# Key norms of the RWKV preparation: one addition and one power for both halves of the features

## The chip, the cores and the metric

The program runs on one core of a Trainium2 chip. The time is that of one execution on the device, in microseconds (us); a kernel's time is the median of its runs. The core's engines work side by side, each through its own list of instructions in a fixed order, and wait for each other through semaphores: TensorE (PE in the profile; PEld are its weight loads), VectorE (DVE), ScalarE (ACT), GpSimd (POOL) and SyncE (SP), which here issues most DMA transfers. The clock of TensorE is not constant: the profile gives, for each stretch, the share of the full clock that was granted.

## What is computed

The reference is one layer of a decoder trunk for 1024 tokens and 16 meta tokens, D_MODEL 1024. An input projection feeds four groups of heads (pooling, RWKV-7, a gated linear recurrence, an mLSTM), each 256 features wide; an output projection and a layer norm follow, then an MLP with a squared ReLU and 4096 hidden features, and a last layer norm. The part that matters here is RWKV's, with 4 heads of 64 features:

```python
def rwkv7_mixer(p, mu, w0, w_up, a0, a_up, g_up, k_k, k_a, r_k, gn_g, gn_b, v_first, v_mix):
    pm = p + (token_shift(p) - p) * mu
    r, k, v, wd, ad, gd = jnp.split(pm, RW_SPLITS, axis=-1)
    w = -jax.nn.softplus(-(w0 + jnp.tanh(wd) @ w_up)) - 0.5
    log_decay = -jnp.exp(w.astype(jnp.float32))
    a = jax.nn.sigmoid(a0 + ad @ a_up)
    ...
    kk = split_heads(k * k_k)
    kk = kk * lax.rsqrt(jnp.sum(kk * kk, -1, keepdims=True) + 1e-12)
    k = k * (1.0 + (a - 1.0) * k_a)
    ...
    bvec = kk * ah
    # step over the tokens: S = S * d - (S kk) b + v k ; y = S r
    ...
    bonus = jnp.sum(rh * kh * r_k, -1, keepdims=True) * vh
    out = (y + bonus.reshape(B, T, GROUP_W)) * g
```

The key norm is the line with `rsqrt`: for each token and head, the sum of 64 squares, plus 1e-12, to the power -0.5. `kk` is multiplied by it.

## The kernel before

Features lie on the 128 partitions and tokens along the free axis, so the 256 features of RWKV are two halves, f = 0 and 1, of 128 partitions, with two heads each. The tokens come in four blocks of 256; block 0 has the 16 meta tokens ahead of them, so 272 columns. Within a block the scan works on chunks of 128 tokens (block 0 has a third chunk, of 16).

All matrix products in float32 are done as three products of rounded parts: a high part (`whi`, made by ScalarE, L127 or L132) and the rest (`wlo`, made by VectorE, L128 or L133). Lines L476 to L478 are the input projection, which the code calls a sweep, L1169 to L1171 the output projection W_out, and L1191 the products of the MLP, whose second half writes to `bank`. L188 are transposes on TensorE.

The program is written as steps in a string (`PLAN`, L41 and below): `P2`, for one, is `rwkv_pre` of block 2, `I2` the inverse of its chunks' triangular matrices, `C2.0` a chunk's scan, `c2.0` that chunk's output (`rwkv_out`), `W2.1` a piece of W_out, `G` and `D` pieces of the MLP. A scheduler takes these steps as priorities and sets the order of the instructions on each engine with costs of its own; so an edit in one step can move instructions of other steps that run near it, and sometimes later ones. Tiles come from pools with a fixed number of buffers: a new tile of a name waits until the last reader of the oldest one of that name is done.

`rwkv_pre` (L604 and below) prepares a block. A first loop over f makes the decays: matmuls L626 and L627, tanh (L633, L638), L634 and the scan L635. A second loop over f does the rest of the half's work:

- L643 multiplies k by its gain (ScalarE), L645 squares it into `rw_s`, and L648 sums the squares over each head on TensorE: the squares are the stationary operand and a matrix of ones (`blk`, 2 columns) the moving one, so that tokens come to lie on partitions and the result is 128x2 for each chunk, 128x4 for the block's two chunks.
- `rsqrt` adds 1e-12 on VectorE (L139) and takes the power -0.5 on GpSimd (L140). In block 0 the meta chunk has an addition and a power of its own, 16x2.
- L657 brings the norm back to features on partitions: a matmul with the norm, broadcast to 64 columns, as its stationary operand and the identity as the moving one. L659 multiplies it into `kk` (VectorE).
- L661 and L662 are exponentials of the decays. L667 and L668 update k (the first writes an `rw_s`), L670 is r times k (another `rw_s`), L672 the matmul that sums it for the bonus, L673 and L674 the bonus. L675 to L683 multiply `kk`, r, k and a by the decays. L694 are the first matmuls behind, of the inverse.

Two things tie these together. `rw_s` has two buffers, and each half takes three in turn: the squares, L667's and L670's. And the tag `r` of PSUM, with two buffers, holds the sums of squares, the broadcast norms and L672's result in turn.

The head norms of the chunks' outputs use `rsqrt` as well (tile `rw_rs`). `rwkv_out` (L887 and below) then transposes the normalised output (L890), multiplies it by the gate's matmul (L892) in L895 and L896 into a tile `ys`, which has one buffer, and sends it to DRAM as `yd` (L591, issued by SP).

## Time and profile before

| | us |
|---|---|
| median of 3 runs | 1275.45 |
| lowest and highest run | 1268.3, 1279.51 |
| the profiled execution | 1273.62 |
| its span, first to last instruction | 1271.8 |
| TensorE busy in the span | 1208.1 |
| VectorE busy | 844.4 |
| ScalarE busy | 594.5 |
| GpSimd busy | 110.1 |

The mean granted clock of TensorE over the span was 0.983 of the full one. A row of a timeline has start, length, engine, line, operation, tiles and shapes, and in brackets the idle time ahead of it and what ended it: `[1.46 <-POOL rw_rn L140]` says that the engine stood still for 1.46 us until GpSimd's power on `rw_rn` was done. A row of the waits has the engine and line that waited, what it waited for, the total, the number of times and the longest. A group's row has shapes, count, busy time in us and mean of one in ns. A row of the windows has the stretch and its length, the busy time and count of each engine (TensorE, its weight loads, VectorE, ScalarE, GpSimd), the granted clock, the share of the DMA engines and GB/s. `rwkv_pre` runs at about 75 us (block 0), 187 (block 1), 481 (block 2) and 586 (block 3).

### The profile page before, as it was taken

The numbers are of one execution on the slowest core, as the hardware profiler recorded it, in microseconds if no ns is written. First come the engines' busy times: TensorE is split into PE (matmuls) and PEld (weight loads), VectorE is DVE, ScalarE is ACT, GpSimd is POOL, SyncE is SP. The second block draws the span as 40 slices with busy tenths as digits, with TensorE's granted clock in tenths as the row PEclk, the third lists the DMA queues.
The fourth block names the chain that finished last, engine by engine and source line by source line (L and its number), as shares of the span: only waits on it lengthen the run. The fifth ranks groups of instructions, "written<-read, shape, count | busy, mean of one in ns | idle before, by whom it ended". The sixth has DMA issues, their size and how long they took to land.

```text
span 1271.8 us, 20464 instructions
## 1 busy us (share of the span) xinstructions
PE 1208.1 (95%) x7642; PEld 1036.5 (81%) x7642; DVE 844.4 (66%) x1834; ACT 594.5 (47%) x989; POOL 110.1 (9%) x124
## 2 busy tenths in 40 slices
PE   4999999899987998999999899999999999999997
PEld 3989878889887996776788787888888888888886
DVE  8856476877743756736766789766765556445687
ACT  5433757354265534344343346655655543343330
POOL 4110010200120000001001330000000000000022
PEclk9999999899998998999999999999999999999999
DMA  7536333984895472565647767666666788666662
GB/s 250 183 106 227 94 124 93 204 202 105 232 285 158 147 291 88 159 157 129 224 117 210 254 228 235 224 233 241 221 237 231 237 296 283 198 192 191 193 220 100
DMA packets 123171, 247.90 MB, mean 195 GB/s; under 512 B 28832, under 2 KB 35632, under 8 KB 122944
## 3 DMA queue, kind: packets, MB, share of 16 engines
q1 hardware_dynamic: 114624, 229.82, 54.3%
q0 software_dynamic: 8448, 16.78, 7.8%
q8 instruction: 60, 0.98, 0.3%
q14 instruction: 39, 0.32, 0.1%
HBM read 195.17 MB, written 84.94 MB: 220 GB/s over the span
## 4 chain that ended last, share of the span: by engine, by line
PE 75%; DVE 8%; DMA 7%; issue 4%; ACT 4%; POOL 2%; SPq 1%; DVEq 0%; ACTq 0%; POOLq 0%
PE bank L1191 39%; PE b L1191 6%; PE b L477 5%; PE b L478 4%; PE b L476 4%; DMA wraw<-in_w_out 2%; DVE wlo L128 2%; PE r L694 2%; PE b L1170 1%; PE b L1169 1%; PE b L1171 1%; DMA wraw<-in_w 1%; ACT whi L127 1%; DMA yd<-ml_num 1%; POOL rw_rn L140 1%
## 5 line engine op out<-in xcount | busy, mean ns | idle before, releaser
L476 PE MATMUL b<-hTh,whi 128*128 128x256 f32 (+1 forms) x672 | 198.2, 295 | 3.2 <-ACT whi L127 2.3
L133 DVE TENSOR_TENSOR wlo<-wraw,whi 128x1024 fp32r<-128x1024 f32 x112 | 133.7, 1227 | 100.0 <-ACT whi L132 97.6
L477 PE MATMUL b<-hTl,whi 128*128 128x256 f32 (+1 forms) x672 | 198.3, 295 | 0.8 <-DVE hTl L133 0.7
L478 PE MATMUL b<-hTh,wlo 128*128 128x256 f32 (+1 forms) x672 | 196.7, 293 | 2.2 <-DVE wlo L128 2.1
L132 ACT CAST whi<-wraw 128x1024 fp32r<-128x1024 f32 x112 | 113.1, 1052 | 162.9 <-PE bank L1191 143.1
L1191 PE MATMUL bank<-whi 128*128 128x512 f32 x448 | 175.0, 392 | 2.6 <-DVE ys L896 2.6
L1191 PE MATMUL bank<-wlo,whi 128*128 128x512 f32 x448 | 175.6, 392 | 1.3 <-DVE wlo L133 1.3
L1191 PE MATMUL bank<-whi,wlo 128*128 128x512 f32 x448 | 175.3, 391 | 0.0
L127 ACT CAST whi<-wraw 128x1024 fp32r<-128x1024 f32 x90 | 94.3, 1048 | 144.5 <-PE b L477 49.6
L128 DVE TENSOR_TENSOR wlo<-wraw,whi 128x1024 fp32r<-128x1024 f32 x90 | 111.0, 1235 | 76.1 <-ACT whi L127 75.6
L476 PEld LDWEIGHTS b<-hTh,whi 128*128 128x128 f32 x672 | 131.6, 196 | 6.2 <-ACT whi L127 2.7
L478 PEld LDWEIGHTS b<-hTh,wlo 128*128 128x128 f32 x672 | 131.8, 196 | 4.5 <-DVE wlo L128 3.2
L477 PEld LDWEIGHTS b<-hTl,whi 128*128 128x128 f32 x672 | 131.7, 196 | 2.9 <-DVE hTl L133 1.4
L1191 PEld LDWEIGHTS bank<-whi 128*128 128x128 f32 x448 | 84.6, 189 | 20.0 <-issue 3.0
L1191 PEld LDWEIGHTS bank<-wlo,whi 128*128 128x128 f32 x448 | 84.5, 189 | 19.1 <-DVE wlo L133 1.9
L1191 PEld LDWEIGHTS bank<-whi,wlo 128*128 128x128 f32 x448 | 84.5, 189 | 17.4
L140 POOL TENSOR_TENSOR ln_rs<-ln_rs,mhalf 128x1 f32<-128x1 f32 (+1 forms) x22 | 32.8, 1495 | 611.1 <-DVE ln_rs L139 611.0
L1170 PE MATMUL b<-wlo,mixh 128*128 128x256 f32 x256 | 74.3, 292 | 3.4 <-DVE wlo L128 3.4
L1169 PE MATMUL b<-whi,mixh 128*128 128x256 f32 x256 | 73.3, 289 | 0.9 <-ACT mixh L132 0.9
L1171 PE MATMUL b<-whi,mixl 128*128 128x256 f32 x256 | 72.6, 287 | 0.0
L1170 PEld LDWEIGHTS b<-wlo,mixh 128*128 128x128 f32 x256 | 48.8, 191 | 6.5 <-DVE wlo L128 5.3
L1191 PE MATMUL b<-h1Th,wlo 128*128 128x512 f32 x128 | 52.3, 411 | 0.5 <-DVE wlo L128 0.5
(435 smaller groups left out, 2480.7 us busy)
## 6 DMA issues: line engine op xcount, KB each, us to landing
wraw<-in_w SPq DMA_DIRECT2D x48, 512.0 KB, 4.7
wraw<-in_w_in SPq DMA_DIRECT2D x42, 512.0 KB, 4.7
rd<-in_w POOLq DMA_DIRECT2D x16, 1024.0 KB, 13.5
wraw<-in_w_out SPq DMA_DIRECT2D x32, 512.0 KB, 4.7
wraw<-rd SPq DMA_DIRECT2D x64, 256.0 KB, 4.3
md<-m SPq DMA_DIRECT2D x48, 256.0 KB, 2.3
wraw<-md SPq DMA_DIRECT2D x48, 256.0 KB, 3.4
wraw<-in_w SPq DMA_DIRECT2D x48, 256.0 KB, 4.1
```

The lines of the kernel that those rows point to most:

```text
L127: nc.scalar.copy(hi, raw)
L128: (nc.gpsimd if pool else nc.vector).tensor_tensor(lo, raw, hi.bitcast(F32), op=ALU.subtract)
L132: self.nc.scalar.copy(hi, src)
L133: self.nc.vector.tensor_tensor(lo, src, hi.bitcast(F32), op=ALU.subtract)
L140: self.last_pool = nc.gpsimd.tensor_tensor(out, out, self.mhalf[0:rows, 0:w], op=ALU.pow).ins
L476: nc.tensor.matmul(pt, lhsT=wh[:, ks], rhs=hh[:, kt, 0:nb], start=(kt == 0), stop=False)
L477: nc.tensor.matmul(pt, lhsT=wh[:, ks], rhs=hl[:, kt, 0:nb], start=False, stop=False)
L478: nc.tensor.matmul(pt, lhsT=wl[:, ks], rhs=hh[:, kt, 0:nb], start=False, stop=(kt == 7))
L1169: nc.tensor.matmul(pt, lhsT=xh, rhs=wh, start=(kt == 0), stop=False)
L1170: nc.tensor.matmul(pt, lhsT=xh, rhs=wl, start=False, stop=False)
L1171: nc.tensor.matmul(pt, lhsT=xl, rhs=wh, start=False, stop=(kt == 7))
L1191: mm = lambda *p, **k: self.nc.tensor.matmul(*p, skip_group_check=True, **k)
```

## The change

The second loop of `rwkv_pre` is cut in two. A new loop over f does L643, the square and the sums of squares for both halves, into one PSUM tile `pn` with a further dimension of 2. Behind it stand one addition and one power for all four heads, into one tile `rw_rn` with 4 columns a chunk (128x8 in a block, 16x4 for block 0's meta chunk). The remaining loop reads its two columns from that tile. Lines behind the change stand one further down (L648 becomes L647, L657 becomes L658, L694 becomes L695).

```diff
--- before.py
+++ after.py
@@ -636,25 +636,26 @@
             cs.append(sg)
 
             nc.scalar.activation(at[:, f, 0:nb], pa, AF.Tanh, scale=0.5, bias=self.hp[:, 2 + f:3 + f])
+        m = 1 if mo else 0
+        pn = self.ps("r", [P, nch, 2, 2])
+        for f in range(2):
+            KK = kk[:, f, 0:nb]
+            nc.scalar.activation(KK, k[:, f, 0:nb], AF.Identity, scale=self.p("kk", f))
+            sq = self.rwp.tile([P, NBM], F32, name="rw_s", bufs=2)
+            nc.scalar.activation(sq[:, 0:nb], KK, AF.Square)
+            for ci, (c0, L, _, _) in enumerate(ch):
+                nc.tensor.matmul(pn[0:L, ci, f], lhsT=sq[:, c0:c0 + L], rhs=self.blk, start=True, stop=True)
+        rn = self.smp.tile([P, NTB + 1, 4], F32, name="rw_rn")
+        for rs, i0, i1 in ([(slice(0, NM), 0, 1)] if mo else []) + [(slice(0, P), m, nch)]:
+            self.rsqrt(rn[rs, i0:i1].rearrange("p a b -> p (a b)"), pn[rs, i0:i1].rearrange("p a b c -> p (a b c)"), 1e-12)
         for f in range(2):
             c = cs[f]
             A = at[:, f, 0:nb]
             K, R, V, KK, BV = (t[:, f, 0:nb] for t in (k, r, v, kk, bv))
-            nc.scalar.activation(KK, K, AF.Identity, scale=self.p("kk", f))
-            sq = self.rwp.tile([P, NBM], F32, name="rw_s", bufs=2)
-            nc.scalar.activation(sq[:, 0:nb], KK, AF.Square)
-            pn = self.ps("r", [P, nch, 2])
-            for ci, (c0, L, _, _) in enumerate(ch):
-                nc.tensor.matmul(pn[0:L, ci], lhsT=sq[:, c0:c0 + L], rhs=self.blk, start=True, stop=True)
-            rn = self.smp.tile([P, NTB + 1, 2], F32, name="rw_rn")
-            m = 1 if mo else 0
-            for rs, i0, i1 in ([(slice(0, NM), 0, 1)] if mo else []) + [(slice(0, P), m, nch)]:
-                o = rn[rs, i0:i1].rearrange("p a b -> p (a b)")
-                self.rsqrt(o, pn[rs, i0:i1].rearrange("p a b -> p (a b)"), 1e-12)
             pb = self.ps("r", [P, nb])
             for ci, (c0, L, _, _) in enumerate(ch):
                 for j in range(2):
-                    nc.tensor.matmul(pb[64 * j:64 * j + 64, c0:c0 + L], lhsT=rn[0:L, ci, j:j + 1].broadcast_to([L, 64]),
+                    nc.tensor.matmul(pb[64 * j:64 * j + 64, c0:c0 + L], lhsT=rn[0:L, ci, 2 * f + j:2 * f + j + 1].broadcast_to([L, 64]),
                                      rhs=self.ident[0:L, 0:L], start=True, stop=True)
             nc.vector.tensor_tensor(KK, KK, pb, op=ALU.mult)
             ep, en = tmp[:, 2], tmp[:, 3]
```

The order of instructions moves at these places. First TensorE, block 2 (about 481 to 489 us in the profile of before): the norm's sums of squares, the broadcasts of the norm, the bonus sums (written into `r`) and the transposes of the MLP's input (L188) between them. Before:

```order
L648 MATMUL r_5789<-cst_280,rw_s_5787 128x2 x2
L188 MATMUL b_6183<-cst_280,x_6174 128x128 x4
L188 MATMUL b_6192<-cst_280,x_6190 128x128
L934 MATMUL l_5860<-cst_280,ml_g_4376 128x8 x2
L188 MATMUL b_6192<-cst_280,x_6190 128x128 x3
L657 MATMUL r_5795<-cst_280,rw_rn_5792 64x128 x4
L672 MATMUL r_5809<-rw_s_5807,bd_rkb_949 128x256
L188 MATMUL b_6199<-cst_280,x_6190 128x128 x4
L648 MATMUL r_5821<-cst_280,rw_s_5819 128x2 x2
L657 MATMUL r_5827<-cst_280,rw_rn_5824 64x128 x4
L672 MATMUL r_5841<-rw_s_5839,bd_rkb_949 128x256
```

And with the change:

```order
L647 MATMUL r_5776<-cst_280,rw_s_5778 128x2 x2
L647 MATMUL r_5776<-cst_280,rw_s_5783 128x2 x2
L188 MATMUL b_6169<-cst_280,x_6160 128x128 x4
L188 MATMUL b_6178<-cst_280,x_6176 128x128
L935 MATMUL l_5846<-cst_280,ml_g_4366 128x8 x2
L188 MATMUL b_6178<-cst_280,x_6176 128x128 x3
L658 MATMUL r_5790<-cst_280,rw_rn_5787 64x128 x4
L673 MATMUL r_5804<-rw_s_5802,bd_rkb_949 128x256
L658 MATMUL r_5813<-cst_280,rw_rn_5787 64x128 x4
L673 MATMUL r_5827<-rw_s_5825,bd_rkb_949 128x256
```

Both halves' sums of squares now stand together ahead of the covering transposes, and one group of four transposes (the one on `b_6199`) no longer stands between the two halves; it comes behind the first eight matmuls of the inverse.

VectorE at the same place. `rw_s` written from `rw_a` is L667 (L668 with the change), `rw_s` from `rw_r` is L670 (L671). Before, between the additions and multiplications of block 2's norm:

```order
L659 TENSOR_TENSOR rw_kk_5760<-rw_kk_5760,r_5795 128x256
L673 TENSOR_TENSOR rw_bv_5762<-r_5809,rw_v_4871 128x256
L675 SCALAR_TENSOR_TENSOR rw_a_5761<-rw_a_5761,rw_kk_5760 128x256
L139 TENSOR_SCALAR rw_rn_5824<-r_5821 128x4
L677 TENSOR_TENSOR rw_kk_5760<-rw_kk_5760,p4_5767 128x256
L683 SCALAR_TENSOR_TENSOR rw_a_5761<-rw_a_5761,p4_5767 128x256
L667 TENSOR_SCALAR rw_s_5836<-rw_a_5761,hp_404 128x256
L659 TENSOR_TENSOR rw_kk_5760<-rw_kk_5760,r_5827 128x256
L668 SCALAR_TENSOR_TENSOR rw_k_4869<-rw_s_5836,rw_k_4869 128x256
L675 SCALAR_TENSOR_TENSOR rw_a_5761<-rw_a_5761,rw_kk_5760 128x256
L670 TENSOR_TENSOR rw_s_5839<-rw_r_4870,rw_k_4869 128x256
```

With the change:

```order
L668 TENSOR_SCALAR rw_s_5799<-rw_a_5751,hp_404 128x256
L944 TENSOR_TENSOR ml_li_5837<-l_5846,ifb_951 128x8
L669 SCALAR_TENSOR_TENSOR rw_k_4859<-rw_s_5799,rw_k_4859 128x256
L660 TENSOR_TENSOR rw_kk_5750<-rw_kk_5750,r_5790 128x256
L671 TENSOR_TENSOR rw_s_5802<-rw_r_4860,rw_k_4859 128x256
L676 SCALAR_TENSOR_TENSOR rw_a_5751<-rw_a_5751,rw_kk_5750 128x256
L680 TENSOR_TENSOR rw_r_4860<-rw_r_4860,p4_5757 128x256
L674 TENSOR_TENSOR rw_bv_5752<-r_5804,rw_v_4861 128x256
L678 TENSOR_TENSOR rw_kk_5750<-rw_kk_5750,p4_5757 128x256
L682 TENSOR_TENSOR rw_k_4859<-rw_k_4859,p4_5757 128x256
L684 SCALAR_TENSOR_TENSOR rw_a_5751<-rw_a_5751,p4_5757 128x256
L660 TENSOR_TENSOR rw_kk_5750<-rw_kk_5750,r_5813 128x256
```

Behind these rows follow, for half 1, L668, L945 (a small one), L669, L676 and L671. What moved in is half 0's own work on k and r: L668, L669, L671, L680 and L682 with `p4_5757`. Before, these five stood some 30 to 70 rows ahead, between input projections; three of them:

```order
L670 TENSOR_TENSOR rw_s_5807<-rw_r_4870,rw_k_4869 128x256
L521 COPY rw_q_5504<-rcar_291 128x1
L521 COPY rw_q_5540<-rcar_291 128x1
L679 TENSOR_TENSOR rw_r_4870<-rw_r_4870,p4_5767 128x256
L681 TENSOR_TENSOR rw_k_4869<-rw_k_4869,p4_5767 128x256
```

The third place is the end of block 3, VectorE at about 691 to 703 us: the last two `rwkv_out` (L895 and L896 on two tiles `ys`), the head norm's addition L139 and multiplication L914, sums of W_out (L1174) and splits of weights (L128). Before:

```order
L895 SCALAR_TENSOR_TENSOR ys_7650<-r_7645,prm_282,rw_bv_6663 128x128
L139 TENSOR_SCALAR rw_rs_7336<-rw_sm_7335 128x4
L895 SCALAR_TENSOR_TENSOR ys_7650<-r_7645,prm_282,rw_bv_6663 128x128
L914 TENSOR_TENSOR rw_yn_7337<-rw_yn_7337,rw_rs_7336 128x256
L896 TENSOR_TENSOR ys_7650<-ys_7650,r_7645 128x256
L1174 SCALAR_TENSOR_TENSOR x_7817<-x_7817,b_7963 128x256
L1174 SCALAR_TENSOR_TENSOR x_7819<-x_7819,b_7964 128x256
L128 TENSOR_TENSOR wlo_8062<-wraw_8059,whi_8061 128x1024
L895 SCALAR_TENSOR_TENSOR ys_7890<-r_7885,prm_282,rw_bv_6663 128x128 x2
L128 TENSOR_TENSOR wlo_8233<-wraw_8230,whi_8232 128x1024
L896 TENSOR_TENSOR ys_7890<-ys_7890,r_7885 128x256
```

With the change:

```order
L896 SCALAR_TENSOR_TENSOR ys_7632<-r_7627,prm_282,rw_bv_6649 128x128 x2
L913 TENSOR_REDUCE rw_sm_7317<-SA_7320 128x4
L897 TENSOR_TENSOR ys_7632<-ys_7632,r_7627 128x256
L139 TENSOR_SCALAR rw_rs_7318<-rw_sm_7317 128x4
L128 TENSOR_TENSOR wlo_8014<-wraw_8011,whi_8013 128x1024
L915 TENSOR_TENSOR rw_yn_7319<-rw_yn_7319,rw_rs_7318 128x256
L1175 SCALAR_TENSOR_TENSOR x_7799<-x_7799,b_7945 128x256
L896 SCALAR_TENSOR_TENSOR ys_7872<-r_7867,prm_282,rw_bv_6649 128x128 x2
L1175 SCALAR_TENSOR_TENSOR x_7801<-x_7801,b_7946 128x256
L897 TENSOR_TENSOR ys_7872<-ys_7872,r_7867 128x256
L128 TENSOR_TENSOR wlo_8044<-wraw_8041,whi_8043 128x1024
L128 TENSOR_TENSOR wlo_8215<-wraw_8212,whi_8214 128x1024
```

The first tile's L897 now stands ahead of the head norm's addition and multiplication, and the last tile's L896 and L897 ahead of both splits of weights. From about 785 us to the end TensorE's order is the one of before.

## The prediction

> **What bounds the kernel now.** I read the page first, then TensorE's waits, then the timeline of each place where one of those waits is for the key norm, and last the windows with the granted clock. The head of the page, the busy shares and the chain by line:
>
> ```profile
> span 1271.8 us, 20464 instructions
> PE 1208.1 (95%) x7642; PEld 1036.5 (81%) x7642; DVE 844.4 (66%) x1834; ACT 594.5 (47%) x989; POOL 110.1 (9%) x124
> PE bank L1191 39%; PE b L1191 6%; PE b L477 5%; PE b L478 4%; PE b L476 4%; DMA wraw<-in_w_out 2%; DVE wlo L128 2%; PE r L694 2%; PE b L1170 1%; PE b L1169 1%; PE b L1171 1%; DMA wraw<-in_w 1%; ACT whi L127 1%; DMA yd<-ml_num 1%; POOL rw_rn L140 1%
> ```
>
> TensorE is busy 1208.1 of 1271.8 us, so all idle time of TensorE in the whole program is 63.7 us, and only work that TensorE waits for can be won or lost. VectorE at 66% and GpSimd at 9% have room. The norm's power (L140 on `rw_rn`) has 1% of the chain. TensorE's waits for it, first in the whole run, then in the windows 66 to 86 us (block 0), 184 to 200 (block 1), 478 to 500 (block 2, with a second wait that stands beside it) and 580 to 600 (block 3); the columns are total, times and longest:
>
> ```profile
> PE r L657 <- POOL rw_rn L140: 5.0, 8, 1.5
> PE r L657 <- POOL rw_rn L140: 1.3, 3, 0.5
> PE r L657 <- POOL rw_rn L140: 1.2, 2, 0.8
> PE r L672 <- DVE rw_s L670: 1.6, 1, 1.6
> PE r L657 <- POOL rw_rn L140: 1.5, 1, 1.5
> PE r L657 <- POOL rw_rn L140: 1.1, 2, 0.7
> ```
>
> So 5.0 us of TensorE's time wait for the powers, and with the wait for L670 in block 2 some 6.6 us, 0.5% of the span. That is the ceiling of what the change can win in these four places; a measurement of this kernel tells about 1% from no change, 12.7 us.
>
> **The change, part by part: the instructions removed.** Per block one addition on VectorE and one power on GpSimd go (in block 0 two of each, because the 16 meta columns have their own). The remaining power has twice the columns: 128x8, in block 0 also 16x4.
>
> ```profile
> L139 DVE TENSOR_SCALAR rw_rn<-r x10: 142/156/163, 74.9 to 590.4; 128x4 f32<-128x4 f32 x8, 16x2 f32<-16x2 f32 x2
> L140 POOL TENSOR_TENSOR rw_rn<-rw_rn,mhalf x10: 692/1144/1492, 75.1 to 590.6; 128x4 f32<-128x4 f32 x8, 16x2 f32<-16x2 f32 x2
> L140 POOL TENSOR_TENSOR rw_rn<-rw_rn,mhalf 128x4 f32<-128x4 f32 x8 | 9.8, 1224 | 45.5 <-DVE rw_rn L139 45.5
> L140 POOL TENSOR_TENSOR ln_rs<-ln_rs,mhalf 128x1 f32<-128x1 f32 x21 | 32.3, 1540 | 610.7 <-DVE ln_rs L139 610.6
> L140 POOL TENSOR_TENSOR ln_rs<-ln_rs,mhalf 16x1 f32<-16x1 f32 x1 | 0.5, 542 | 0.4 <-DVE ln_rs L139 0.4
> ```
>
> Five additions of 0.156 us (0.8 us of VectorE) and five powers of about 1.1 us (5.5 us of GpSimd) go. Both engines have idle time around them, so this pays only through the waits. The trace has no 128x8 power. It is bounded from below by one 128x4, 1.22 us, and from above by two of them, 2.45. Width seems to cost something among the short ones (16x1 takes 0.54, the shortest of all, a 16x2, 0.69: 0.15 a column), and nothing in the 128x1, which at 1.54 is longer than the 128x4. I take 1.6: the 128x4 and four columns at 0.1, below the slope of the short ones because of the 128x1 row. The 16x4 gets 0.69 + 2 x 0.15 = 1.0.
>
> [...]
>
> **Block 0.** TensorE's norm matmuls (L648), the first cover behind them, and the two broadcasts of half 0:
>
> ```profile
> 74.13 0.74 PE L648 MATMUL r<-cst,rw_s 128*16 128x2 f32 x6
> 74.73 0.37 PE L476 MATMUL b<-hTh,whi 128*128 128x272 f32 x1
> 75.88 0.29 PE L657 MATMUL r<-cst,rw_rn 16*64 16x16 f32 x4 [0.41 <-POOL rw_rn L140]
> 77.35 0.66 PE L657 MATMUL r<-cst,rw_rn 128*64 128x128 f32 x8 [0.53 <-POOL rw_rn L140]
> ```
>
> Before, three waits make 1.3, two of them here. The first power (0.69) ended at 75.88, so it began 0.46 behind the norms. After, both halves' L647 stand together (0.6 us each, to 75.3); the powers then run from 75.8 to 76.8 (16x4) and 78.4 (128x8). Six matmuls cover the norm where four took from 74.73 to 75.47, 0.74 us; six make 1.1, to 76.4. The waits are then 0.4, and, behind a broadcast of 0.3, 1.3: 1.7 against 1.3. The second half's broadcasts wait for nothing. **+0.4 us**, ends 0 (the powers at 1.2) and +1.2 (at 2.45).
>
> **Block 1.** Two waits (1.2 together, the longer 0.8) become one, longer by the power's 0.4: 0.8 + 0.4 = 1.2. The order of ScalarE here gets one more table load, of the length of the first row below, in a stretch whose idle time just behind is the second row's 1.12:
>
> ```profile
> 188.62 1.28 ACT L1092 ACT_TABLE_LOAD   x1
> 197.96 0.47 ACT L1092 ACTIVATE sc<-l,prm 128x256 f32<-128x256 f32 x1 [1.12 <-PE l L1091]
> ```
>
> The 1.12 hide all but 0.2 of the 1.28: **+0.2 us**, ends -0.4 (a short power, the load hidden) and +1.3 (the load not hidden).
>
> **Block 2.** Here half 0's work on K, r and the bonus (L667, L668, L670, L679, L681) ran early in the old order, since the two `rw_s` buffers were free for it. Now both buffers hold squares until the norm matmuls have read them, so these five operations stand behind the norm, in VectorE's stream between the two halves. The old filling work, the old stalls and VectorE's pace:
>
> ```profile
> 483.94 0.60 PE L188 MATMUL b<-cst,x 128*128 128x128 f32 x4
> 486.34 0.66 PE L657 MATMUL r<-cst,rw_rn 128*64 128x128 f32 x8 [1.46 <-POOL rw_rn L140]
> 488.62 1.15 PE L672 MATMUL r<-rw_s,bd_rkb 128*128 128x256 f32 x2 [1.62 <-DVE rw_s L670]
> 483.52 0.42 DVE L659 TENSOR_TENSOR rw_kk<-rw_kk,r 128x256 f32<-128x256 f32 x1 [0.36 <-PE r L657]
> 487.04 0.42 DVE L659 TENSOR_TENSOR rw_kk<-rw_kk,r 128x256 f32<-128x256 f32 x1 [1.03 <-PE r L657]
> 488.05 0.42 DVE L670 TENSOR_TENSOR rw_s<-rw_r,rw_k 128x256 f32<-128x256 f32 x1
> ```
>
> From 487.04 to 488.05 three operations start, 0.335 us apart. Before, the second L670 set the second L672 at 488.62. After, the first broadcast comes 0.4 later (the longer power), so the first L660 is at about 483.95. From it to the second L671 the new order has thirteen full operations and one small, like the addition: 12 x 0.335 + 0.16 + 0.42 = 4.6, which ends at 488.55. So the second wait for the power is gone, but VectorE arrives when it did: the stall changes its releaser, not its end. What differs is that the four transposes (L188, 0.6 us), which filled TensorE between the halves, now stand behind both: **+0.6 us**, ends 0 (VectorE keeps ahead) and +1.5 (the power at 2.45).
>
> **Block 3.** Two waits (0.7 and 0.4) become one of 0.7 + 0.4: **0**.
>
> **The tail of block 3.** From about 690 us the planner writes W_out, the down products and the last two `rwkv_out` in another order. VectorE's rows, SP's issue and TensorE's wait:
>
> ```profile
> 692.93 0.43 DVE L914 TENSOR_TENSOR rw_yn<-rw_yn,rw_rs 128x256 f32<-128x256 f32 x1 [0.90 <-POOL rw_rs L140]
> 693.27 0.42 DVE L896 TENSOR_TENSOR ys<-ys,r 128x256 f32<-128x256 f32 x1
> 693.72 0.38 SPq L591 DMA_DIRECT2D yd<-ys  x1
> 700.33 0.61 DVE L895 SCALAR_TENSOR_TENSOR ys<-r,prm,rw_bv 128x128 f32<-128x128 f32 x2 [4.84 <-DMA yd<-ys]
> 700.97 1.23 DVE L128 TENSOR_TENSOR wlo<-wraw,whi 128x1024 fp32r<-128x1024 f32 x1
> 702.67 0.47 PE L1191 MATMUL bank<-whi 128*128 128x512 f32 x1 [2.56 <-DVE ys L896]
> ```
>
> The single `ys` buffer is sent out at 693.72 and free at 700.33, 6.6 us later. VectorE then does L895, a weight split (1.23) and L896, and TensorE waits 2.56 us for that. In the new order the earlier tile's product comes ahead of the wait for the head norm's power (0.90 + 0.34 sooner), and the last product ahead of the split (1.23; a sum of W_out, as long as an L914, takes its place: 0.8 sooner): 2.0 of 2.56 us. The down product that waited now also has more W_out matmuls ahead of it, but the loads on SP move with it, so I take **-1.5 us**, ends 0 and -2.6.
>
> Sum: 0.4 + 0.2 + 0.6 + 0 - 1.5 = -0.3. Against the profiled execution's 1273.62 us (span 1271.8 and 1.8 around it) that is 1273.3. The median of the three runs is 1275.45, 1.8 above the profiled one, and they spread from 1268.3 to 1279.51, wider than any term here.
>
> **The rivals.** Two rest on the clock, so first its rows: 488 to 492 us, 492 to 496, 496 to 500, and 704 to 707; the clock is the number ahead of the last two.
>
> ```profile
> 488.00:492.00 4.00, 3.14 (x10) 1.97 (x10) 3.33 (x11) 0.88 (x3) 0.00 (x0) 0.58 0.00 0
> 492.00:496.00 4.00, 3.73 (x19) 3.51 (x20) 2.03 (x8) 2.03 (x6) 0.00 (x0) 0.50 0.12 22
> 496.00:500.00 4.00, 4.00 (x15) 2.89 (x14) 3.35 (x13) 1.45 (x3) 0.00 (x0) 0.64 0.38 108
> 704.00:707.00 3.00, 3.00 (x8) 2.31 (x7) 2.96 (x6) 0.98 (x1) 1.27 (x1) 0.50 0.63 206
> 703.45 0.40 PE L1191 MATMUL bank<-whi 128*128 128x512 f32 x1
> 703.68 0.59 PE L1191 MATMUL bank<-wlo,whi 128*128 128x512 f32 x1
> 704.50 0.63 PE L1191 MATMUL bank<-whi 128*128 128x512 f32 x1
> 704.92 0.63 PE L1191 MATMUL bank<-wlo,whi 128*128 128x512 f32 x1
> ```
>
> After block 2's two stalls the clock is at half for about 3.4 + 4 + 2.9 = 10.2 us; after the tail's stall for some 3.4. A 512-column matmul then starts every 0.42 us instead of 0.23, so half of the time is lost at most: 1.6 us in the short stretch, 4.7 in the long one.
>
> *Slower: the merged waits bring the clock down elsewhere.* In blocks 0, 1 and 3 a single longer wait stands where there were two or three short ones. Block 2's stalls, 3.1 us within 4 us, were followed by half clock. If a merged wait of 1.1 to 1.3 us in one piece does the same, each of three blocks pays 1.6: 1278.1. It decides where such a wait comes near block 2's 3.1 us; at the forecast lengths it stays below. For over 1% it would need three stretches as long as block 2's. Chance 0.17.
> [...]
>
> *Slower: width is paid in full.* The power at 2.45, 0.85 more in four waits: 3.4 us, 1276.7. For it speaks only the slope of the short forms, against it the 128x1 row. Chance 0.13.
>
> *Faster: the half-clock stretches go with their stalls.* The tail's wait vanishes wholly (1.1 more) and with it the stretch at 704 (1.6), and block 2's stretch too (4.7): 1265.9. For it: both stretches follow stalls that the new order moves. Against it: in block 2 VectorE still ends at 488.5. Chance 0.2.
>
> **How the numbers follow.** My forecast, no difference that shows, 1273.3, has 0.5 (its own range 1270 to 1277). The range reaches to the faster rival with a power at its lower bound in three blocks (0.4 each), 1264.7, rounded to 1265, and to both slower ones together with half of the tail's gain lost, 1282; outside I leave 2 in 10 at most, the spread of the runs included. Faster by over 1% (under 1262.7) needs the fast rival and a further 3.2 us: 0.07. Slower by over 1% (over 1288.2) needs long half-clock stretches in three blocks: 0.06. The rest, 0.87, is within 1%.
>
> **What would show it.** Right: five powers on `rw_rn`, the 128x8 at 1.2 to 2.0 us; TensorE's total wait for them 4 to 6 us in some five pieces, not eight; in block 2 the second bonus matmul still waits for VectorE until about 488.5 and the half clock follows; near 700 us the wait for `ys` falls below 1.5. Wrong: new half-clock stretches behind blocks 0, 1 or 3, a power near 2.5 us, or a shift of many microseconds at a place without a norm, which this argument does not reach.

## The result: 1.4% slower

Over four executions each, the changed kernel takes 1292.38 us in the median (1288.05 to 1295.67) and the kernel before 1272.78 (1268.3 to 1279.51). The ratio is 1.0142, with an interval of 1.0104 to 1.0180. The forecast of 1273.3 us is missed by 19, and all four executions lie outside its range.

The head of the page of the changed kernel, its profiled execution taking 1288.05 us:

```profile
span 1286.2 us, 20446 instructions
PE 1216.9 (95%) x7642; PEld 1042.3 (81%) x7642; DVE 845.1 (66%) x1829; ACT 597.6 (46%) x990; POOL 104.0 (8%) x119
```

The span is 14.4 us longer. The five additions and five powers are gone (VectorE 1834 to 1829 instructions, GpSimd 124 to 119). TensorE does the same 7642 matmuls, but is busy 8.8 us longer (1208.1 to 1216.9): the same work at a mean granted clock of 0.978 against 0.983. The other 5.6 us are new idle time (63.7 to 69.3). The largest of TensorE's waits that bear on the change, whole run (total, times, longest):

```profile
PE r L658 <- POOL rw_rn L140: 6.0, 5, 1.8
PE r L822 <- DVE PQ L836: 4.7, 1, 4.7
PE r L673 <- DVE rw_s L671: 3.6, 2, 2.7
```

The first and third were forecast. The second is a single wait of 4.7 us in the intra-chunk inverse, which has no norm in it.

To find where the 14.4 us arise, each matmul of one trace was matched with the same matmul of the other, and the difference of their starts, the shift, followed along the program. Where it rises, the changed kernel loses time. The median shifts, worked out from the two traces:

| stretch, us in the trace before | shift at its ends, us | change | forecast |
|---|---|---|---|
| 0 to 60, start of the program | 0 to 0.9 | +0.9 | none |
| 60 to 100, block 0's norm | 0.9 to 4.95 | **+4.0** | +0.4 |
| 165 to 180, ahead of block 1's norm | 4.95 to 5.5 | +0.5 | none |
| 180 to 240, block 1's norm | 5.5 to 8.0 | **+2.5** | +0.2 |
| 340 to 420 | 8.0 to 5.1 | -2.9 | none |
| 470 to 530, block 2's norm | 5.1 to 5.6 | +0.5 | +0.6 |
| 530 to 545 | 5.6 to 4.4 | -1.2 | none |
| 545 to 565, inverse of block 2's first chunk | 4.4 to 11.1 | **+6.7** | none |
| 570 to 650, block 3 | 11.1 to 12.9 | +1.9 | 0 |
| 650 to 785, tail of block 3 | 12.9 to 12.4 | -0.5 | -1.5 |
| 800 to 1000, MLP | 12.4 to 14.4 | +2.0 | none |

Three stretches hold 13.2 of the 14.4 us. The 0.5 near 170 us arises in unchanged code, where VectorE waits 1.72 us for a transfer (`sc` to `yd`), 1.19 before. The fall at 340 to 420 is a stretch of half clock that the execution before happened to have at 393 to 403 us. The rise at 800 to 1000 also stands in most other kernels below, among them one whose order there is that of before; its cause stays open.

**Block 0.** The changed kernel's TensorE from the norm's sums of squares to the first matmuls behind the broadcasts (start, length of one, line; in brackets the wait ahead of it), with five covering matmuls left out:

```profile
75.06 1.41 PE L647 MATMUL r<-cst,rw_s 128*16 128x2 f32 x12
76.34 0.38 PE L476 MATMUL b<-hTh,whi 128*128 128x272 f32 x1
...
79.15 0.29 PE L658 MATMUL r<-cst,rw_rn 16*64 16x16 f32 x4 [1.80 <-POOL rw_rn L140]
80.76 1.12 PE L658 MATMUL r<-cst,rw_rn 128*64 128x128 f32 x8 [1.32 <-POOL rw_rn L140]
...
82.20 0.43 PE L477 MATMUL b<-hTl,whi 128*128 128x272 f32 x1
```

The two waits make 3.1 us where 1.7 were forecast. What was mis-sized is the first power. The groups of GpSimd on `rw_rn` (busy, mean ns of one), and VectorE's row beside the first:

```profile
L140 POOL TENSOR_TENSOR rw_rn<-rw_rn,mhalf 128x8 f32<-128x8 f32 x4 | 6.9, 1737 | 46.8 <-DVE rw_rn L139 46.8
L140 POOL TENSOR_TENSOR rw_rn<-rw_rn,mhalf 16x4 f32<-16x4 f32 x1 | 2.4, 2351 | 20.3 <-DVE rw_rn L139 20.3
77.01 1.21 DVE L128 TENSOR_TENSOR wlo<-wraw,whi 128x1024 fp32r<-128x1024 f32 x1
```

The 128x8 takes 1.74 in the mean (forecast 1.6), but the 16x4 took 2.35 instead of 1.0. It began at 76.74, and VectorE's split of a weight ran beside it from 77.01 to 78.22. A run below shows that this neighbour is the cause.

Windows of 4 us, first of the kernel before (76 to 88 us), then of the changed one (the same, and 196 to 200 in block 1). TensorE's busy time is the second number, the granted clock stands ahead of the last two:

```profile
76.00:80.00 4.00, 3.47 (x30) 2.67 (x30) 2.02 (x6) 0.52 (x1) 1.30 (x1) 1.00 0.44 133
80.00:84.00 4.00, 3.62 (x32) 3.08 (x33) 2.19 (x10) 1.22 (x3) 2.00 (x2) 1.00 0.00 0
84.00:88.00 4.00, 4.00 (x27) 3.27 (x27) 3.83 (x14) 0.95 (x2) 0.00 (x0) 1.00 0.02 4
```

```profile
76.00:80.00 4.00, 1.63 (x14) 1.31 (x14) 2.37 (x7) 0.48 (x2) 3.26 (x2) 0.95 0.19 49
80.00:84.00 4.00, 3.24 (x17) 2.91 (x18) 1.65 (x6) 0.00 (x0) 0.70 (x1) 0.50 0.21 84
84.00:88.00 4.00, 4.00 (x27) 3.39 (x27) 1.09 (x4) 1.00 (x3) 0.00 (x0) 0.69 0.00 0
196.00:200.00 4.00, 4.00 (x25) 2.82 (x21) 2.33 (x7) 0.83 (x3) 0.42 (x4) 0.61 0.01 2
```

Before, the clock is whole through all of block 0's norm. After, it is at half from about 80 us on, for some 7 us. The waits for the power grew from 1.3 to 3.1, which is 1.8 of the 4.0 us; the other 2.2 are put down to the clock. In block 1 a single wait of 1.19 us at 195.5 is followed by the same: 0.61 in the last row, where before has 1.00.

**Block 2's inverse.** The stretch with the 6.7 us. First the changed kernel: GpSimd's issue of two accumulating transfers of the MLP (`rd`), SP's issue of the loads of which the first is MLP step 8's (`wraw`), ScalarE's cast, VectorE's split between the copies on `AT` and those on `PQ`, and TensorE:

```profile
543.46 2.13 POOL L1223 DMA_DIRECT2D rd<-in_w  x2
549.49 1.32 SPq L124 DMA_DIRECT2D wraw<-in_w  x2
562.77 1.04 ACT L127 CAST whi<-wraw 128x1024 fp32r<-128x1024 f32 x1 [5.98 <-DMA wraw<-in_w]
557.32 0.77 DVE L832 COPY_PREDICATED AT<-msk,r 128x256 f32<-128x256 uint8 x2 [1.80 <-PE r L695]
563.85 1.23 DVE L128 TENSOR_TENSOR wlo<-wraw,whi 128x1024 fp32r<-128x1024 f32 x1 [5.76 <-ACT whi L127]
564.99 1.33 DVE L836 COPY_PREDICATED PQ<-msk,r 128x512 f32<-128x512 uint8 x2
565.77 0.69 PE L822 MATMUL r<-cst,rw_k 128*128 128x128 f32 x2 [4.67 <-DVE PQ L836]
```

The same load, transfers, cast, split and copies in the kernel before:

```profile
536.46 0.34 SPq L124 DMA_DIRECT2D wraw<-in_w  x1
539.59 2.12 POOL L1222 DMA_DIRECT2D rd<-in_w  x2
547.41 1.05 ACT L127 CAST whi<-wraw 128x1024 fp32r<-128x1024 f32 x1
548.79 1.23 DVE L128 TENSOR_TENSOR wlo<-wraw,whi 128x1024 fp32r<-128x1024 f32 x1
553.41 0.77 DVE L831 COPY_PREDICATED AT<-msk,r 128x256 f32<-128x256 uint8 x2 [2.04 <-PE r L694]
555.23 1.34 DVE L835 COPY_PREDICATED PQ<-msk,r 128x512 f32<-128x512 uint8 x2 [0.69 <-PE r L694]
```

Before, the planner had put this split ahead of the copies on `AT`. The changed order puts it between them and the copies on `PQ`. The copies on `PQ` stand behind it in VectorE's stream and started at 564.99, as it ended. The load took 13 us from issue to cast, so 5.8 us of VectorE and then 4.7 of TensorE went by on a weight that nobody yet needed.

The load is late because its place among SP's transfers moved too. In the kernel before it was issued 3.1 us ahead of the accumulating transfers and landed after 4.0 us, 6.9 us ahead of its cast; it is matched to this cast by the semaphore that the cast waits for. With the change it is issued 6.0 us behind them, and the first of its packets moves at 556 us. This is not peculiar to the changed order: in the kernel before, the next two loads were issued behind the accumulating transfers, at 543.66 and 550.04, and moved nothing before 554 us. Which of the transfers in flight held these loads back, the accumulating ones or those ahead of them on SP's queue, is not separated.

**Block 2's norm and the tail.** TensorE's waits in the changed kernel, from 478 to 505 us and from 690 to 715:

```profile
PE r L673 <- DVE rw_s L671: 3.6, 2, 2.7
PE r L658 <- POOL rw_rn L140: 0.7, 1, 0.7
PE b L1171 <- DVE wlo L128: 1.4, 1, 1.4
PE b L1170 <- ACT whi L127: 0.3, 1, 0.3
```

In block 2 VectorE took the stall over, as forecast. In the tail the wait for `ys` (2.56) is gone, and waits for weights of 1.7 stand in its place.

### The profile page after: what moved, and what is told of

The parts are those of the page before. It is cut to its first block, busy times and chain, and to the rows that moved or that the text cites. A ratio compares the mean times of both kernels' runs of the same rounds, so it can differ in the third digit from the quotient of the medians.

```text
span 1286.2 us, 20446 instructions
## 1 busy us (share of the span) xinstructions
PE 1216.9 (95%) x7642; PEld 1042.3 (81%) x7642; DVE 845.1 (66%) x1829; ACT 597.6 (46%) x990; POOL 104.0 (8%) x119
## 4 chain that ended last, share of the span: by engine, by line
PE 74%; DMA 9%; DVE 8%; ACT 3%; issue 3%; POOL 2%; SPq 1%; DVEq 0%; ACTq 0%; POOLq 0%
PE bank L1192 38%; PE b L1192 5%; PE b L477 5%; PE b L478 5%; PE b L476 5%; DMA wraw<-in_w 2%; PE r L695 1%; DMA yd<-ys 1%; PE b L1171 1%; PE b L1170 1%; DVE wlo L128 1%; PE b L1172 1%; DMA wraw<-in_w_out 1%; DMA x<-yd 1%; DMA yd<-ml_num 1%
## 5 line engine op out<-in xcount | busy, mean ns | idle before, releaser
L128 DVE TENSOR_TENSOR wlo<-wraw,whi 128x1024 fp32r<-128x1024 f32 x90 | 110.5, 1230 | 83.3 <-ACT whi L127 83.1
L140 POOL TENSOR_TENSOR ln_rs<-ln_rs,mhalf 128x1 f32<-128x1 f32 (+1 forms) x22 | 29.7, 1351 | 606.5 <-DVE ln_rs L139 606.4
L1192 PE MATMUL b<-h1Th,whi 128*128 128x512 f32 x128 | 52.6, 416 | 0.6 <-ACT p L1207 0.4
```

The costliest lines, as they stand in the source:

```text
L128: (nc.gpsimd if pool else nc.vector).tensor_tensor(lo, raw, hi.bitcast(F32), op=ALU.subtract)
L140: self.last_pool = nc.gpsimd.tensor_tensor(out, out, self.mhalf[0:rows, 0:w], op=ALU.pow).ins
L1192: mm = lambda *p, **k: self.nc.tensor.matmul(*p, skip_group_check=True, **k)
```

## Experiments

All kernels below compute the same. For them the norm is written as a loop over groups of halves, with the rest of a half in a function of its own. The group list `[(0, 1)]` for all blocks gives the changed kernel's order on every engine, `[(0,), (1,)]` that of the kernel before. All ratios are to the kernel before on the same chip, with their intervals.

### One block at a time

The loop's list names the block in which the norm is merged; here block 0 (the kernel only_b0), and in the same way blocks 1, 2 and 3:

```diff
-        for g in [(0, 1)]:
+        for g in ([(0, 1)] if b == 0 else [(0,), (1,)]):
```

> The merged norm in block 0 alone, blocks 1 to 3 as before. Theory (the merged wait): TensorE waits about 3.1 us in two pieces at the norm of block 0 (1.3 before), half clock follows for 5 us, and everything behind 95 us is 4.0 us later than in the kernel before: some 1276 to 1278 against 1273. Rival (the loss sits elsewhere: a tenth of the whole at each place, or only the clock's luck): no shift at 95 us beyond 1 us, time equal to before within 0.2%. Either way the order of the blocks behind is that of before, so the wait of 4.7 us near 561 us is absent.

> The merged norm in block 1 alone. Theory (the merged wait and half clock): one wait of about 1.2 us for the power, a stretch of half clock of 3.4 us behind it, one more table load; 3 us later from 240 us on, some 1276. Rival (block 1's own part is the clock's phase and not the wait): the wait is there, the clock stays full, shift within 0.7 us.

> The merged norm in block 2 alone. Theory (a reordered weight split): at the norm itself, 480 to 500 us, the shift is within 1 us; near 556 us TensorE waits about 4.7 us for the PQ copies behind the split of the weights of MLP step 8, whose load crosses the accumulating transfers, half clock follows, shift 5 to 7 us from 570 us on: about 1279 to 1280. Rival (the five operations of half 0 behind the norm are what costs): the shift stands at 480 to 500 us already, 2 us or more, and the wait near 556 us is short.

> The merged norm in block 3 alone. Theory: the longer merged wait costs 1 to 2 us between 580 and 640 us, no half clock; 1274 to 1275. Rival (the tail's order, forecast as a gain of 1.5): the shift at 785 us is -1 us or less.

Measured: block 0 alone 1.0035 (1.0003 to 1.0067), block 1 alone 1.0058 (1.0030 to 1.0087), block 2 alone 1.0072 (1.0035 to 1.0109), block 3 alone 1.0013 (0.9983 to 1.0043). The four parts add up to 1.78%, give or take 0.64 (root of the squares of the half widths, although all four share the runs of the kernel before), against 1.42% for all together.

Block 0 alone shifts by 4.1 us in its own stretch (1.1 to 5.2), with half clock from 80 to 87 us (0.50 and 0.65 in the windows from 80 to 88). Block 1 alone shifts by 2.3 at its norm, with half clock behind a wait of 1.2 (0.64 from 200 to 204); a further 7.5 came earlier, at 140 to 180, in unchanged code. So its norm shows 2.3 of the 7.4 us that the timed rounds put on block 1; where the rest arises is open. Block 2 alone has the wait far from its norm:

```profile
PE r L830 <- DVE PQ L844: 3.0, 1, 3.0
```

Its shift is 1.6 us at 530, 0.4 at 545, and 6.0 at 580. So the split moved because of block 2's norm, 70 us ahead of it in the program, and the load with it: issued at 545.63, 6.2 us behind the accumulating transfers, cast at 557.09. Block 3 alone costs 0.2 us at its own norm. Its profiled execution lost 8.7 us between 550 and 565 us, where its order is that of before, with a wait of 1.4 and half clock behind it: a single execution can move by that much at a place whose order is that of before, and the timed rounds have the last word.

### The split behind the copies

The changed kernel, with step 8's cast and split put in the order behind the `PQ` copies and the copy of `G` of block 2's first chunk; only the order is changed, there is no new semaphore (the kernel late_g8):

```diff
+        cp = nc.scalar.copy(G[0:L], pg[0:L, 0]).ins
+        if (b, ci) == (2, 0):
+            self.late = (self.pq, cp)
...
+            for x in self.late if k == 8 else ():
+                st.enter_context(self.tc.issue_after(x))
             wh, wl = self.load_w(self.a["w1"][k])
```

> The change as it is, and the weight split (cast on ScalarE, rest on VectorE) of the MLP's step 8 queued behind the PQ copies and the copy of G of block 2's first chunk. Theory (that split, waiting for its load, holds the copies): TensorE's wait for PQ near 561 us falls from 4.7 us below 0.5, no half clock follows there, the shift against before at 575 us is 4 to 7 us instead of 11 to 13.6; time some 6 us under the change's, 1.009 of before. Rival (the load or the transfers themselves hold TensorE): another wait of 4 us or more takes its place within 20 us and the time stays at 1.014.

Measured: 1.0063 (1.0038 to 1.0089). VectorE's two rows:

```profile
559.29 1.34 DVE L844 COPY_PREDICATED PQ<-msk,r 128x512 f32<-128x512 uint8 x2 [1.04 <-PE r L703]
562.51 1.22 DVE L128 TENSOR_TENSOR wlo<-wraw,whi 128x1024 fp32r<-128x1024 f32 x1 [1.87 <-ACT whi L127]
```

The load and the split are still late (cast at 561.43), but nothing that TensorE needs stands behind them: the wait for `PQ` is gone, and the shift from 545 to 565 us goes from 4.5 to 4.8 instead of 11.1. The kernel is 0.8% (0.3 to 1.2) faster than the changed one. In the traces 6.4 us (0.5%) of that arise at this one place in VectorE's order, not quite half of the loss; the rest comes later, between 570 and 750 us, where the planner's order moved as well. The swap, the two kernels with narrow powers and the first kernel of the early norm below keep this repair.

### What of block 0 is the power, what its neighbour

The 128x8 power ahead of the 16x4 one:

```diff
-        parts = ([(slice(0, NM), 0, 1)] if mo else []) + [(slice(0, P), m, nch)]
+        parts = [(slice(0, P), m, nch)] + ([(slice(0, NM), 0, 1)] if mo else [])
```

> The merged norm with the late split, and in block 0 the 128x8 power ahead of the meta chunk's 16x4. The broadcast of the meta chunk is still TensorE's first, so it waits for both powers: one wait of about 3 us in place of 1.8 and 1.3. If the length of a wait in one piece decides on the clock, half clock of 3.4 us or more follows as before; if the idle share of a few us decides, the same. Shift at 95 us 3.5 to 5 us in both; a shift under 2 us would say that the half clock in block 0 was the phase's luck.

Measured: 1.0065 (1.0036 to 1.0093), as late_g8. (The same line stands in the mLSTM's preparation and was swapped there too; only small operations move by that.) GpSimd's two powers in block 0, by shape, and TensorE's wait:

```profile
L140 POOL TENSOR_TENSOR rw_rn<-rw_rn,mhalf 128x8 f32<-128x8 f32 x1 | 3.0, 2974 | 20.3 <-DVE rw_rn L139 20.3
L140 POOL TENSOR_TENSOR rw_rn<-rw_rn,mhalf 16x4 f32<-16x4 f32 x1 | 1.0, 1002 | 0.0
79.58 1.45 PE L666 MATMUL r<-cst,rw_rn 16*64 16x16 f32 x12 [3.30 <-POOL rw_rn L140]
```

Now the 128x8 stands beside the split and takes 2.97 (in the changed kernel's block 0 it took 1.63), and the 16x4, behind the split, takes 1.00 instead of 2.35. In both orders the power that came first, beside the split, took about 1.35 longer, a little more than the split's 1.21. So this order only changes who pays; the wait is 3.3 in one piece, and the half clock (0.50 from 80 to 84 us) and a shift of 4.2 are the same.

In the changed kernel the power shows as started at 76.74, before the split at 77.01, and yet it was the one that took longer; the split's 1.21 is that of VectorE's other splits (1.23 in the mean of 90). The profile's times of GpSimd are rough, so the order of the two starts is not certain. Nor was every power beside a split slowed by as much: in the kernel before, the first 16x2 ran from 75.14 on, with a split beside it from 75.20, and took 0.69, the shortest of its width; the 128x4 behind it took 1.49, where the shortest is 1.00. What in the two operations makes a power take longer is not shown.

### Two narrow powers behind the squares

Squares of both halves first, as in the change, but an addition and a power for each half, into a tile for each:

```diff
-            for rs, i0, i1 in parts:
-                self.rsqrt(rn[rs, i0:i1].rearrange("p a b -> p (a b)"), pn[rs, i0:i1].rearrange("p a b c -> p (a b c)"), 1e-12)
+            for f in g:
+                for rs, i0, i1 in parts:
+                    self.rsqrt(rn[f][rs, i0:i1].rearrange("p a b -> p (a b)"), pn[rs, f, i0:i1].rearrange("p a b -> p (a b)"), 1e-12)
```

> As the run before, but the norms keep an addition and a power for each half (squares of both halves first, 128x4 twice instead of 128x8 once). Theory (the merged power and the wait in one piece): the first broadcast of a block comes 0.4 us sooner in blocks 1 to 3 and about 1.8 sooner in block 0; block 0's shift falls from 4.0 to 1 or 2 us, its half clock goes; 2 to 4 us under the run before. Rival (squares first and the two square buffers are what costs, the power's merging is not): blocks 0 and 1 keep their shifts of 4 and 3 to 5 us; time within 1 us of the run before.

Measured: 1.0025 (0.9992 to 1.0058). Waits for the power fall to 3.6 us in four pieces (6.2 in five in late_g8), and block 0 shifts by 2.2 instead of 4.1. Its half clock is not gone, as the theory had it, but shorter: 3.4 us behind waits of 1.6 and 0.7 (0.66 and 0.92 in the windows from 76 to 84). Block 1 still shifts by 3.1 at its norm, with half clock (0.59 from 190 to 194). In the trace the result lies between the two theories: width costs something, but a part of the loss stays with narrow powers, so it belongs to the order. The timed rounds do not decide it: the interval reaches from no loss to most of late_g8's, and the difference of 0.4% to late_g8 is about as large as its uncertainty.

The same with the squares written into the bonus tile, so that the buffers of `rw_s` stay free for half 0's work:

```diff
-                sq = self.rwp.tile([P, NBM], F32, name="rw_s", bufs=2)
+                sq = bv[:, f]
```

> As the run before, and the squares are written into the bonus tile, which is free until later, so both buffers of rw_s stay with the halves' own work, which may run ahead of the norm as in the kernel before. If the buffers are what costs: VectorE's half-0 work leaves the stretch behind the norm, blocks 1 and 2 lose their shifts, and the time is that of before, 1.000 within 0.004. If the order of squares costs by itself: 1.004 to 1.009.

Measured: 1.0215 (1.0165 to 1.0266), the slowest of all, against both theories. The planner made a different order over most of the program, with TensorE waiting 8.0 us for `rw_yn` and 4.3 for cast weights in places that the edit does not name. What the two `rw_s` buffers cost therefore stays open.

### A wait of one microsecond by itself

The kernel before, with one short GpSimd multiplication by ones (0.52 us) ahead of the power of block 1's first half. No width and no merging, only a later power; TensorE's order differs there by one covering matmul:

```diff
+            self.twice = b == 1 and g == (0,)
...
+        if getattr(self, "twice", False):
+            self.twice = False
+            nc.gpsimd.tensor_tensor(out, out, self.ones8[0:rows, 0:w], op=ALU.mult)
```

> The kernel before, with one more GpSimd instruction (a multiplication by ones, 128x4) ahead of the power of half 0 in block 1; the order on every other engine stays, but for one covering matmul that moves ahead of the wait. Only the wait grows: from 0.8 us in one piece to some 1.2 to 1.8. Theory (a single wait of more than about a microsecond brings the clock to half for 3.4 us): half clock between about 190 and 196 us, shift there 2 to 3 us. Rival (the clock falls by its own phase, or only after waits of 3 us in all, as behind block 2's norm): the clock stays at 1.00 there and the shift is 0.4 to 1.0 us.

The wait, and the windows of 4 us from 188 to 200:

```profile
191.40 1.04 PE L672 MATMUL r<-cst,rw_rn 128*64 128x128 f32 x8 [1.09 <-POOL rw_rn L143]
188.00:192.00 4.00, 2.90 (x21) 2.25 (x21) 1.72 (x5) 3.33 (x8) 1.62 (x2) 0.94 0.63 219
192.00:196.00 4.00, 4.00 (x20) 3.49 (x18) 2.76 (x9) 1.56 (x3) 1.12 (x6) 0.50 0.02 4
196.00:200.00 4.00, 4.00 (x25) 3.39 (x24) 1.45 (x4) 3.08 (x5) 0.62 (x1) 0.71 0.00 0
```

A single wait of 1.09 (the longest there was 0.8 in the kernel before) is followed by half clock for more than 4 us. The shift, already 1.8 us from unchanged code near 171 us, goes from 1.8 to 4.8 between 187 and 196 us: 3.0 us for this wait and its half clock, as the theory had it.

Over the timed rounds, though, the kernel is at 1.0001 (0.9972 to 1.0031). An interval of 0.3% holds 3.0 us, and two other kernels (only_b0 and, below, the one with the early norm in blocks 0 and 3), whose block 1 has the old norm with waits of up to 0.8 us, ran at half clock there in the profiled execution too (0.76 and 0.82 from 194 to 202, 0.64 and 0.50 from 190 to 198), while the kernel before had 1.00. So behind waits near one microsecond the clock was down in some executions and not in others, and in block 1 the kernel before may already pay for it some of the time.

### The norm earlier

To take the wait away and keep the wide power: the merged norm moves ahead of the loop over the decays, so that more work stands between the power and its reader.

```diff
+        g = (0, 1)
+        pn = self.ps("r", [P, nch, len(g), 2])
+        for i, f in enumerate(g):
...
+            self.rsqrt(rn[rs, i0:i1].rearrange("p a b -> p (a b)"), pn[rs, i0:i1].rearrange("p a b c -> p (a b c)"), 1e-12)
         for f in range(2):
...
-        for g in [(0, 1)]:
-            pn = self.ps("r", [P, nch, len(g), 2])
...
+        for f in range(2):
+            self.rwkv_half(rw, b, f, f, ch, rn, tmp, cs[f], w0, W, m)
```

> The merged norm (one addition, one power for a block) with the late split, and the squares, their sums, the addition and the power moved ahead of the decays' loop in each block, so that the matmuls, tanh and scans of the decays stand between the norm and its broadcast. Theory (what costs in blocks 0, 1 and 3 is the merged wait): TensorE's waits for the power fall from 6 us to under 2, blocks 0 and 1 lose their shifts of 4 and 2 to 4 us down to 1 or less, and the time is within 0.3% of before. Rival (an order made anew loses as much at other places): waits for the power gone, time still 1.005 or more.

Measured: 1.0014 (0.9990 to 1.0039), against 1.0063 for late_g8. TensorE no longer waits for the power in any block. In block 0 the windows from 76 to 84 us:

```profile
76.00:80.00 4.00, 3.80 (x25) 2.56 (x24) 2.75 (x10) 2.03 (x7) 3.61 (x2) 1.00 0.32 116
80.00:84.00 4.00, 3.99 (x38) 3.07 (x36) 3.88 (x13) 1.84 (x8) 0.00 (x0) 1.00 0.05 17
```

GpSimd is as slow as before (3.61 in the fifth busy number), but TensorE is busy and the clock whole; block 0 shifts by 0.7 us instead of 4.0. This is the strongest evidence for block 0: the same two powers, no wait, no half clock, almost no loss. From 165 to 205 us, block 1's preparation and norm, the kernel still shifts by 2.8, now with waits of 1.3 for VectorE (`sc`) and 1.7 for ScalarE, and block 2's second bonus sum still waits 3.1.

Then only in blocks 0 and 3, with the old norm in 1 and 2, and only in block 3:

```diff
+EARLY = (0, 3)
...
+        if b in EARLY:
```

> The merged norm ahead of the decays' loop in blocks 0 and 3, blocks 1 and 2 as before (the split of MLP step 8 stays where it was before). Theory (a norm that nothing waits for gains what the kernel before loses there, 1.3 and 1.1 us): TensorE's waits for the power fall from 5.0 to about 2.7 us; shift at 95 us and at 640 us between -1.5 and +0.7; time 0.998 to 1.001 of before. Rival (a new order costs as much elsewhere): 1.002 or more.

> The same in block 3 alone. Theory: TensorE's wait of 1.1 us for the power in block 3 goes, shift between 570 and 640 us -1 to 0; time 0.999 to 1.0. Rival: 1.002 or more.

Measured: 1.0010 (0.9975 to 1.0046) and 1.0034 (1.0000 to 1.0067). Neither beats the kernel before. The first cuts the waits for the power from 5.0 to 2.3 us in all, and gets nothing measurable for it; the second shows half clock in block 3, 0.80, 0.50, 0.50 and 0.92 in the windows from 588 to 604 us. No version tried is faster than the kernel before.

### The clock over all traced executions

| place | half clock behind the norm |
|---|---|
| block 0, merged norm in its changed place | 4 of 4 |
| block 0, old norm | 0 of 6 |
| block 0, squares first with narrow powers | 2 of 2 |
| block 0, merged norm ahead of the decays | 0 of 2 |
| block 1, merged norm in its changed place | 4 of 4 |
| block 1, old norm | 2 of 6 |
| block 1, old norm with the longer wait | 1 of 1 |

Block 0's rows are without exception, so its cost is the change's. In block 1 part of the cost is there before.

The length of a single wait does not decide it. The kernel before waits 1.30 us in one piece for a weight near 782 us, and the clock stays whole; the changed one waits 1.39 at 711.85, with the clock at 1.00 from 711 to 715.

```profile
781.95 0.50 PE L1191 MATMUL bank<-wlo,whi 128*128 128x512 f32 x1 [1.30 <-DVE wlo L133]
780.00:784.00 4.00, 2.70 (x12) 1.90 (x11) 3.93 (x6) 2.09 (x4) 0.00 (x0) 1.00 0.56 182
784.00:788.00 4.00, 4.00 (x19) 3.18 (x18) 3.93 (x6) 4.00 (x8) 0.00 (x0) 1.00 0.78 259
```

In each of the 14 traces the granted clock changes only on a grid of 3.41 us, which lies differently against the program in each execution: in the kernel before, half clock begins at 222.4, 236.1 and 488.7 us, 4 and 74 steps apart; in the changed one at 79.6 and 195.7 us, 34 steps apart and some 0.6 us off the other's grid. Counted over all traces from 50 to 1245 us, by TensorE's idle time (as the profile has it) within one step at whole clock: with more than 1.8 us idle the next step was at half clock 42 times of 42, with 1.0 to 1.8 us 36 times of 112, with less 22 times of 4565. The merged norm of block 0 puts 2.0 to 2.4 us of idle time into one step, so its half clock is no chance. That of block 1 puts 1.18 there; in its place half clock came each time, but elsewhere such a step is followed by it in fewer than half of the cases.

## Why the prediction was wrong

- **Block 0, +0.4: mis-sized.** It measured +4.0. The count of covering matmuls and the width of the 128x8 power were right. Missing was the split beside the 16x4 power (1.35 us, shown by the swap), which made the waits 3.1 instead of 1.7, and the half clock that follows (2.2 us by the difference above). At 3.1 us the clock rival's own condition, a wait near block 2's 3.1, was met. The early norm shows that without the wait both go.
- **Block 1, +0.2: mis-sized.** The wait came out as forecast, at 1.19 against 1.2; with the half clock behind it the norm shifts by 2.5 us in the trace, and by 2.3 with block 1 changed alone.
- **The clock rival was given 0.17 and was right in two blocks of three.** The sentence that failed is "at the forecast lengths it stays below". In block 0 the length itself was wrong, 3.1 instead of 1.7. In block 1 it was right, and the point from which a wait decides was wrong: block 2's 3.1 us was the one such stretch quoted, but waits of 1.09 and 1.19 were followed by half clock there. The trace before shows the clock whole behind 1.30 us in one piece, so a length of one wait could not have been the measure; the idle time within a step of 3.41 us is the better one (over 1.8 us, 42 times of 42).
- **Block 2's norm, +0.6: right.** It measured +0.5, and the second bonus sum waits for VectorE as the count of operations said.
- **Block 3, 0: right for the norm,** +0.2 where it was changed alone. The 1.9 us of the table are not from the norm's wait, which is 1.0.
- **The tail, -1.5: mis-sized.** The wait for `ys` went, but 1.7 us for weights took its place; -0.5 remained. With block 0 alone changed, and the tail's order that of before, the shift falls by 1.4 there as well, so it is open whether the tail won anything.
- **The place not looked at.** The 6.7 us between 545 and 565 are the largest single loss, and the prediction names only the kind ("a place without a norm, which this argument does not reach"). What failed is the step from the orders to the sum: the split moved between the copies on `AT` and on `PQ`, and its load behind the accumulating transfers, and this place has no term.
- **Power width: right.** 1.63 to 1.96 for the 128x8, 6.0 us of waits in five pieces. The rival with the full 2.45 is out. The 128x1 row that was held against the width is a mean over powers from 0.55 to 3.55 us in the trace before; the short ones take as long as the 16x1. What lengthens the others was not tested; the longest, at 1226.13, ran beside two of VectorE's splits, at 1226.92 and 1228.06.

## What to carry to other kernels

When a change goes through a planner, read the whole difference of the orders, above all where an engine's stream now has an operation that hangs on a load ahead of one that the bound engine needs: here a split that waited 5.8 us made TensorE wait 4.7. Price new idle time of TensorE as its length plus, where more than 1.8 us of it fall within 3.41 us (half clock followed 42 times of 42 in these traces), a stretch at half clock, here 2 to 3 us (2.2 in block 0, 2.5 in block 1); between 1.0 and 1.8 us the half clock followed 36 times of 112. Merging small operations saved here on engines that had time to spare (VectorE busy 66%, GpSimd 8%) and made one longer wait out of two short ones (1.19 us in block 1, where the longest was 0.8); with its result asked for later, the waits for it were gone, and the kernel took 1.0014 of the time before (0.9990 to 1.0039), against 1.0063 with the norm in its changed place.

## What the hardware showed unexpectedly

A power on GpSimd took about 1.35 us longer where a VectorE split of 128x1024 (1.21 us) ran beside it in block 0 of two kernels: 2.35 against 1.00 for the 16x4, 2.97 against 1.63 for the 128x8. The shortest power of each width took 0.54, 0.69, 1.00 and 1.63 us for 1, 2, 4 and 8 columns, about 0.16 us for each further column. The granted clock changed only on a grid of 3.41 us in the 14 traces; a step with more than 1.8 us of idle time on TensorE was followed by one at half clock 42 times of 42, and half clock also stood behind single waits of 1.09 us (wait_b1) and 0.8 us (only_b0). A 512 KB load issued 3 us ahead of two accumulating transfers of 1 MB landed after 4.0 us; issued 6 us behind them, with other transfers between, its reader started 13 us after its issue.
